# RWKV chunk scan: the next tile's matrix doubling interleaved with this tile's sequential chunks

## The chip, the cores and the metric

The kernel runs on all eight cores of one Trainium2 chip. Each core works through four of the 32 sequences, with no traffic between cores. The metric is the device time of the slowest core in microseconds (us), lower is better. The runs fall into a faster and a slower state: in the slow one a die (cores 0 to 3, or 4 to 7) shows a lower granted TensorE clock and a longer span. In the profiled run of the kernel before, cores 0 to 3 took 20,421 us at clock 0.680 and cores 4 to 7 20,189 us at 0.702 (medians), 1.2% apart. Where I compare stages inside the program, I use the mean over all eight cores of a profiled run.

Engine names: PE is TensorE, PEld its weight loads, DVE is VectorE, ACT is ScalarE. PSUM (`ps_B` in the rows) is the memory that matmuls write; DVE and ACT copy results out of it (a 64x384 copy took 0.49 us on ACT and 0.56 on DVE in the tile shown below). The granted clock is the share of TensorE's full clock that the profile's clock records give. They hold three values: on core 0 in the first profile of the kernel before, 1.0 (full) for 5,502 us, 0.5 (half) for 11,978 us and 0.8125 for 2,877 us.

## The reference, cut to what matters

The model is a two-layer trunk of width 1024 on 2048 tokens. Each layer has three mixers side by side (RWKV-7, retention, band attention), an output projection, and a gated convolution FFN. Only the RWKV mixer's recurrence is concerned here:

```python
def step(state, inp):
    r_t, w_t, k_t, v_t, a_t, b_t = inp
    sa = jnp.einsum('bhvk,bhk->bhv', state, a_t)
    state = (state * w_t[:, :, None, :] + sa[..., None] * b_t[:, :, None, :]
             + v_t[..., None] * k_t[:, :, None, :])
    return state, jnp.einsum('bhvk,bhk->bhv', state, r_t)
```

There are six heads of width 64. The kernel does not step token by token. It takes 64 tokens (a chunk) at a time, inverts a triangular matrix for each chunk, and carries the state from chunk to chunk.

## The kernel before

A block of 512 tokens is four tiles of 128 tokens, two chunks in each. For each tile the scan has three stages in this order. The head pairs (hp) are three, the heads in a pair (hh) two. B[0] to B[7] are the eight PSUM banks. A helper records every instruction and derives waits from the buffers and whole banks that it reads and writes. In the chunks, R sums the right-hand sides, SA multiplies them by N (the inverted matrix), ST is what the chunk adds to the state, and Y is its output.

```python
for t_ in range(NT):
    for hp in range(3):                      # mask stage
        ...                                  # 6 matmuls into B[0..3]
        for hh in range(2):
            tt("dve", LM[hp]..., B[hh][:], msk4[:], ALU.mult, ...)
            tt("dve", LT[hp]..., B[2 + hh][:, 0:128], mskL[:, 0, :], ALU.mult, ...)
        tt("dve", nv, lmv[:, :, 0, :], identbf..., ALU.add, ...)
    bnb = [(7, 0), (7, 256), (3, 256)]
    for lev in range(1, 6):                  # doubling: X -> X*X, N -> N + X*N
        for hp in range(3): ...              # squarings into B[4 + hp]
        for hp in range(3):
            cp("dve" if hp == 1 else "act", xx.ap, B[4 + hp][:], ...)
        for hp in range(3): ...              # N products into bnb[hp]
        for hp in range(3):
            tt("dve", nv, nv, B[bn][:, c0n:c0n + 256]..., ALU.add, ...)
    for hf in range(2):                      # two chunks, one after the other
        ...                                  # R: 12 matmuls into B[7]
        cp("act", rhs_sb.ap[tsl, 0:384], B[7][tsl, 0:384], ...)
        ...                                  # SA: 6 matmuls into B[6]
        cp("dve", sa_sb.ap[tsl, 0:384], B[6][tsl, 0:384], ...)
        ...                                  # ST: 12 matmuls into B[2 + hf]
        ...                                  # Y: 18 matmuls into B[5]
        for hp in range(3):
            stt(S32[l][:, hp, :], ..., B[bsn]..., ...)        # state update, DVE
        put_state(Sn)                        # state to bf16, two ACT copies
        for hp in range(3):
            cp("act", yw[hp]..., B[5]..., ...)
```

The softmax here doesn't subtract the row's maximum and nothing guards it: scores larger than these inputs give would overflow.

## Time and profile before

| what | value | from |
|---|---|---|
| time, 20 runs | 20,485.26 us median (20,262.63 to 20,589.65) | timed runs, among them six of 20,466 us median |
| one scan (first mask multiply to the first head-norm matmul after it) | 111.2 us | trace, mean over 8 cores x 32 scans |
| tile to tile in it | 27.5 us | the same |
| time outside, a pair of successive gaps between scans (one of each layer) | 1046.6 us | the same |
| half clock, share of the scan | 84% | clock records, 8 cores |

One whole tile in the busy table reads as follows (stretch, its length, then busy us and count of PE, PEld, DVE, ACT, POOL; then the granted clock, the DMA share and GB/s):

```profile
7286.22:7313.41 27.19, 18.37 (x198) 12.63 (x198) 16.67 (x45) 8.80 (x22) 0.00 (x0) 0.58 0.01 2
```

PE is busy 68% of it and DVE 61%, so two engines have a third of the tile free. PE's own rows of the second chunk show where its third goes. The bracket is the idle time before the row and what ended it:

```profile
7308.80 0.77 PE L283 MATMUL ps_B<-sb_A 128*64 128x64 bf16 x11 [1.65 <-ACT sb_A L309]
7310.29 0.69 PE L283 MATMUL ps_B<-sb_A 128*64 128x64 bf16 x7 [0.73 <-ACT sb_A L309]
7311.61 1.80 PE L283 MATMUL ps_B<-sb_A 64*64 64x64 bf16 x34 [0.62 <-DVE sb_A L311]
```

Three groups, three waits, and each wait is for a copy that itself waited for PE. From the end of ACT's or DVE's work to PE's start it took 0.14 us at nearly every hand-off of the tile that I followed (once 0.25). These are the holes that the change is meant to fill.

### The profile page before, as it was taken

The numbers are of one execution on the slowest core, as the hardware profiler recorded it, in microseconds if no ns is written. First come the engines' busy times: TensorE is split into PE (matmuls) and PEld (weight loads), VectorE is DVE, ScalarE is ACT, GpSimd is POOL, SyncE is SP. The second block draws the span as 40 slices with busy tenths as digits, with TensorE's granted clock in tenths as the row PEclk, the third lists the DMA queues.
The fourth block names the chain that finished last, engine by engine and source line by source line (L and its number), as shares of the span: only waits on it lengthen the run. The fifth ranks groups of instructions, "written<-read, shape, count | busy, mean of one in ns | idle before, by whom it ended". The sixth has DMA issues, their size and how long they took to land.

```text
span 20427.0 us, 232694 instructions; the slowest of 8 cores (20180.5 to 20427.0 us)
## 1 busy us (share of the span) xinstructions
PE 12774.4 (63%) x69184; PEld 6459.9 (32%) x69792; DVE 10440.2 (51%) x17416; ACT 7718.5 (38%) x18017; POOL 874.5 (4%) x1032
## 2 busy tenths in 40 slices
PE   5666566665666666666556666666655666666665
PEld 2323333232332333323333233332333323333232
DVE  5544554455554455445554445544555544554455
ACT  3343333333334333333333433333333343333333
POOL 0000000000000000000000000000000000000000
PEclk7776666777667666667666766667776676666777
DMA  2243322333224332233322433223332243322332
GB/s 51 46 70 52 57 37 46 67 56 57 40 43 69 52 57 36 46 64 56 55 43 42 70 52 56 37 46 64 54 56 45 42 70 52 57 37 46 64 56 49
DMA packets 1045448, 1069.84 MB, mean 52 GB/s; under 512 B 22912, under 2 KB 990592, under 8 KB 1044224
## 3 DMA queue, kind: packets, MB, share of 16 engines
q0 software_dynamic: 991808, 885.52, 29.2%
q1 hardware_dynamic: 52416, 169.40, 2.5%
q8 instruction: 597, 9.78, 0.2%
q14 instruction: 627, 5.14, 0.1%
HBM read 1906.73 MB, written 33.55 MB: 95 GB/s over the span
## 4 chain that ended last, share of the span: by engine, by line
PE 47%; DVE 19%; issue 14%; ACT 10%; DMA 9%; DVEq 1%; ACTq 0%; SPq 0%; POOLq 0%; POOL 0%
PE ps_B L283 45%; DMA sb_W<-w_up 6%; DVE sb_A L295 5%; ACT sb_A L309 4%; DVE sb_xres L295 3%; ACT sb_xres L292 2%; PE ps_B L286 2%; ACT sb_A L290 2%; DMA sb_W<-w_down 2%; DVE sb_A L304 1%; DVE sb_st L367 1%; DVE sb_st L366 1%; DVE sb_A L311 1%; DMA sb_W<-w_in 1%; ACT sb_A L292 1%
## 5 line engine op out<-in xcount | busy, mean ns | idle before, releaser
L283 PE MATMUL ps_B<-sb_xT,sb_W 128*128 128x512 bf16 x16992 | 4711.0, 442 | 1085.6 <-DMA sb_W<-w_up 810.0
L309 ACT ACTIVATE sb_A<-ps_B 128x512 f32<-128x512 f32 (+6 forms) x5440 | 2436.9, 470 | 4222.6 <-PE ps_B L283 3361.2
L283 PE MATMUL ps_B<-sb_A 64*64 64x64 bf16 (+3 forms) x29952 | 2912.7, 267 | 1617.3 <-DVE sb_A L295 589.4
L283 PEld LDWEIGHTS ps_B<-sb_xT,sb_W 128*128 128x128 bf16 x17408 | 1903.8, 111 | 3894.2 <-issue 2914.9
L304 DVE SCALAR_TENSOR_TENSOR sb_A<-sb_A,sb_cw 128x512 f32<-128x512 f32 x2816 | 2092.4, 750 | 1383.3 <-ACT sb_chal L309 1225.0
L283 PEld LDWEIGHTS ps_B<-sb_A 64*64 64x64 bf16 (+2 forms) x29952 | 1974.1, 134 | 2559.4 <-issue 2333.3
L286 PE MATMUL ps_B<-sb_ident,sb_xres 128*128 128x128 f32 x2560 | 580.8, 403 | 1992.2 <-DVE sb_xres L295 1992.2
L295 DVE TENSOR_TENSOR sb_A<-sb_A 128x512 f32<-128x512 f32 (+1 forms) x2240 | 1476.2, 687 | 495.9 <-ACT sb_A L290 372.4
L283 PE MATMUL ps_B<-sb_W,sb_A 128*128 128x512 bf16 x5504 | 1338.4, 405 | 67.3 <-DMA sb_W<-w_down 51.1
L290 ACT ACTIVATE sb_A<-ps_B 128x128 bf16<-128x128 f32 (+2 forms) x2688 | 872.7, 330 | 1054.8 <-PE ps_B L283 1048.3
L295 DVE TENSOR_TENSOR sb_A<-sb_A,ps_B 128x256 bf16<-128x256 bf16 (+1 forms) x2112 | 826.6, 441 | 782.6 <-PE ps_B L283 771.9
L286 PEld LDWEIGHTS ps_B<-sb_ident,sb_xres 128*128 128x128 f32 x2560 | 467.4, 210 | 2124.2 <-issue 2124.2
L292 ACT ACTIVATE sb_A<-ps_B,sb_cb,sb_cw 128x512 f32<-128x512 f32 x1408 | 1072.5, 762 | 1.7
L311 DVE CAST sb_A<-ps_B 128x512 bf16<-128x512 f32 (+3 forms) x1024 | 619.3, 605 | 865.6 <-PE ps_B L283 692.9
L290 ACT ACTIVATE sb_A<-sb_A 128x512 f32<-128x512 f32 (+1 forms) x1344 | 820.8, 624 | 402.5 <-DVE sb_A L295 287.1
L292 ACT ACTIVATE sb_sd<-sb_mv,sb_epst 128x1 f32<-128x1 f32 x320 | 94.2, 294 | 2295.7 <-DVE sb_mv L368 2295.3
L283 PE MATMUL ps_B<-sb_A,sb_bonesbf 128*128 128x512 bf16 x192 | 107.3, 593 | 1250.6 <-DVE sb_A L304 626.0
L283 PE MATMUL ps_B<-sb_W,sb_yT 128*128 128x512 bf16 x1984 | 550.7, 436 | 537.9 <-DVE sb_yT L295 535.5
L304 DVE SCALAR_TENSOR_TENSOR sb_s_0<-sb_xres,ps_B 128x512 f32<-128x512 f32 x256 | 175.4, 685 | 1366.7 <-PE ps_B L283 1357.9
L500 DVE RECIPROCAL sb_rc<-ps_B 128x4 f32<-128x4 f32 x128 | 23.3, 182 | 1625.9 <-PE ps_B L283 1625.9
L283 PEld LDWEIGHTS ps_B<-sb_W,sb_A 128*128 128x128 bf16 x5632 | 578.0, 103 | 824.6 <-issue 467.9
L134 POOL DMA_DIRECT2D sb_W<-w_up x384 | 335.7, 874 | 9803.3 <-PE ps_B L283 9803.3
(100 smaller groups left out, 13822.3 us busy)
## 6 DMA issues: line engine op xcount, KB each, us to landing
sb_W<-w_up POOLq DMA_DIRECT2D x320, 1024.0 KB, 10.8
sb_W<-w_in POOLq DMA_DIRECT2D x224, 768.0 KB, 8.0
sb_W<-w_down POOLq DMA_DIRECT2D x128, 1024.0 KB, 11.2
sb_W<-w_out POOLq DMA_DIRECT2D x64, 1024.0 KB, 10.9
sb_W<-w_down POOLq DMA_DIRECT2D x64, 768.0 KB, 8.9
sb_lng_t<-lng SPq DMA_DIRECT2D x80, 512.0 KB, 4.7
sb_lnb_t<-lnb SPq DMA_DIRECT2D x80, 512.0 KB, 5.7
sb_W<-w_in POOLq DMA_DIRECT2D x32, 1024.0 KB, 9.8
```

Of the source, the lines that this page charges most:

```text
L134: fn = lambda e, out=out, in_=in_: e.dma_start(out=out, in_=in_)
L283: mk.op("pe", lambda e: e.matmul(out, lhsT=lhsT, rhs=rhs, start=start, stop=stop), reads=r, writes=w)
L286: mk.op("pe", lambda e: e.transpose(out, in_, idn), reads=r, writes=w)
L290: mk.op("act", lambda e: e.activation(out=out, in_=in_, func=func, scale=scale), reads=r, writes=w)
L292: mk.op("act", lambda e: e.activation(out=out, in_=in_, func=func, bias=bias, scale=scale), reads=r, writes=w)
L295: mk.op(eng, lambda e: e.tensor_tensor(out=out, in0=in0, in1=in1, op=op), reads=r, writes=w)
L304: mk.op("dve", lambda e: e.scalar_tensor_tensor(out=out, in0=in0, scalar=scalar, in1=in1, op0=op0, op1=op1), reads=r, writes=w)
L309: mk.op("act", lambda e: e.activation(out=out, in_=in_, func=AF.Copy), reads=r, writes=w)
L311: mk.op(eng, lambda e: e.tensor_copy(out=out, in_=in_), reads=r, writes=w)
L366: mk.op("dve", lambda e: e.bn_stats(out=st_[:, 0, :], in_=s_ap[:, 0:512]), reads=[s_key], writes=[k_])
L367: mk.op("dve", lambda e: e.bn_stats(out=st_[:, 1, :], in_=s_ap[:, 512:1024]), reads=[s_key], writes=[k_])
L500: mk.op("dve", lambda e, POv=POv: e.reciprocal(out=rc[:], in_=POv[:, :, 64:65]), reads=[POk], writes=["rc"])
```

## The change

The intent: while the chunks of tile t hop from engine to engine, let PE, ACT and DVE work on the doubling of tile t+1, which does not depend on them. The three stages become a function and two generators. A small driver takes one step of each generator in turn, and that order is the order of issue.

```diff
+LMs = [LM, [alias_bf(f[6], 0, 2), ...]]     # second set of buffers, on dead ones
+LTs = [LT, [...]]
+Nms = [Nm, [...]]
+def mat(t_): ...                            # mask stage, as before
+def gen_dbl(t_):                            # yields after: squarings, copies, N products, N adds
 ...
-  bn, c0n = bnb[hp]
+  bn = 4 + hp                               # N product in the squaring's own bank
 ...
+def gen_seq(t_):                            # yields after each of 8 steps of a chunk
 ...
-  mm(B[6][tsl, ...], nv..., rhs_sb..., ...)  # SA
+  mm(B[7][tsl, ...], nv..., rhs_sb..., ...)
-  o_ = B[5][po:po + 64, ...]                 # Y
+  o_ = B[0][po:po + 64, ...]
 ...
+def run_interleaved(gens): ...              # next() on each in turn until all are done
+mat(0)
+run_interleaved([gen_dbl(0)])
+for t_ in range(NT):
+    if t_ + 1 < NT:
+        mat(t_ + 1)
+        run_interleaved([gen_seq(t_), gen_dbl(t_ + 1)])
+    else:
+        run_interleaved([gen_seq(t_)])
```

The banks had to be dealt out anew, as two stages are alive at once: doubling keeps 4 to 6, chunks take 7, 2 or 3, and 0.

## The prediction

> **What bounds the kernel now.** I read the first lines of the page, then the busy times by stretch, then the timeline of each engine over one step of the RWKV scan, because the change touches nothing else.
>
> ```profile
> span 20427.0 us, 232694 instructions; the slowest of 8 cores (20180.5 to 20427.0 us)
> PE 12774.4 (63%) x69184; PEld 6459.9 (32%) x69792; DVE 10440.2 (51%) x17416; ACT 7718.5 (38%) x18017; POOL 874.5 (4%) x1032
> ```
>
> No engine is full over the whole. The program runs 4 sequences x 4 blocks x 2 layers = 32 layer-blocks, each with one scan of four 128-token tiles. The first mask multiply (sb_msk on DVE) of a scan starts it and the first head-norm matmul (sb_bones on PE) after it ends it. Over all 32 scans of this core that gives 111.06 us a scan (109.7 to 112.3), 3554 us in all, **17.4% of the span**. So the change can only act on 17.4%, and 2% of the time (409 us) means 12.8 us a scan. Tile to tile is 27.46 us in the mean, and the end of the last tile to the first head-norm matmul adds 1.2 us.
>
> Busy times in one tile (stretch in us, then us and count of PE, PEld, DVE, ACT, POOL; then the granted clock). The rows are the mask stage, the doubling, and the two sequential chunks:
>
> ```profile
> 7286.22:7291.68 5.46, 4.04 (x22) 2.05 (x23) 5.46 (x17) 1.77 (x6) 0.00 (x0) 0.50 0.00 0
> 7291.68:7303.32 11.64, 8.59 (x76) 6.08 (x77) 8.24 (x21) 4.88 (x9) 0.00 (x0) 0.67 0.01 2
> 7303.32:7313.41 10.09, 5.74 (x101) 4.50 (x101) 2.97 (x10) 2.15 (x7) 0.00 (x0) 0.52 0.01 2
> ```
>
> The mask stage is DVE bound (5.46 of 5.46). In the chunks nobody is: DVE 2.97 and ACT 2.15 of 10.09. That is a chain of hand-offs. The timeline (start, length, engine, operation) of ACT and then DVE in the second chunk shows it:
>
> ```profile
> 7309.66 0.49 ACT L309 ACTIVATE sb_A<-ps_B 64x384 bf16<-64x384 f32 x1 [0.53 <-PE ps_B L283]
> 7313.51 0.81 ACT L309 ACTIVATE sb_A<-sb_S_1 64x192 bf16<-64x192 f32 x2 [3.36 <-DVE sb_S_1 L304]
> 7314.35 0.46 ACT L309 ACTIVATE sb_A<-ps_B 128x64 f32<-128x64 f32 x3
> ...
> 7310.90 0.56 DVE L311 CAST sb_A<-ps_B 64x384 bf16<-64x384 f32 x1 [3.15 <-PE ps_B L283]
> 7312.37 1.05 DVE L304 SCALAR_TENSOR_TENSOR sb_S_1<-sb_S_1,sb_pcs,ps_B 128x64 f32<-128x64 f32 x3 [0.91 <-PE ps_B L283]
> ```
>
> With the PE rows: right-hand-side matmuls R (12) at 7308.80, ACT copy at 7309.66, SA matmuls (6) at 7310.29, DVE copy at 7310.90, state matmuls ST (12) at 7311.61, state update at 7312.37, state to bf16 at 7313.51 until 7314.32. The hand-offs are R to copy 0.87, copy end to PE 0.14, SA to copy 0.60, ST to update 0.77. A chunk is thus 0.87+0.49+0.14+0.60+0.55+0.14+0.77+1.05+0.10+0.81+0.14 = 5.66 us.
>
> [...] The three rows above agree that there is room: doubling plus chunks have 11.2 us of DVE in 21.7. [...] I lay the streams out by hand in that order. [...] The clock records of this trace hold only 0.5 and 1.0, and average 0.575 in the scans. [...]
>
> **The change part by part.**
> (a) No arithmetic is added or removed: the same matmuls, copies and adds per tile. ACT and DVE work is only reordered, the PE stream too.
> (b) A second set of mask and doubling buffers lies on dead projection buffers. No copies or transfers come from it.
> (c) The mask stage of tile t+1 moves ahead of the chunks of tile t. It still takes 5.5 us of DVE, but the first chunk's R can start when PE has issued the last mask matmuls, some 4.4 us after the first mask multiply (the third pair's matmuls wait for the second pair's banks, read out at about 3.7 us, plus 0.7). So 1.1 us of it hides.
> (d) The N product moves into the squaring's own bank, so the next squaring now waits for the N add. Alone, a level is then S, copy, N, add in a ring. The last head pair needs matmuls 0.44, hand-off 0.18, copy 0.60, 0.15, matmuls 0.22, 0.2, add 0.36, 0.15 = 2.3 us, with queueing about 2.45. Before, N adds start 2.79, 2.41, 2.23 and 1.96 us apart in this tile. So the unhidden first doubling stays about as it was.
> (e) The overlap. Eight steps of a chunk meet eight steps of doubling, that is two levels. PE's order is R, S, SA, N, ST, S, Y, N. Half clock, 0.11 us per 128-column matmul, R at 0:
> - R 0 to 0.77, S to 2.1. Copy of R 0.87 to 1.36, squaring copies ACT 1.39 to 1.99 and 2.28 to 2.88, DVE 1.84 to 2.53.
> - SA waits behind S: 2.1 to 2.5. DVE copy 2.7 to 3.25, N adds 3.25 to 4.33.
> - ST 3.39 to 4.1. Second S to 5.43. Its DVE copy stands ahead of the state update in DVE's queue: 5.17 to 5.86.
> - Y 5.43 to 6.5. Update 5.86 to 6.9, state to bf16 7.0 to 7.8, next R at 7.95. The second N adds end at 8.03, no hindrance.
>
> So a chunk stretches from 5.66 to **7.95 us** (0.6 from SA behind S, 1.7 from the update behind the second copy) and carries two levels, worth 4.9 us alone.
> (f) The fifth level has no partner: chunks have 16 steps, doubling 20. Laid out the same way it adds 2.3 us.
>
> Tile period after: 4.4 + 7.95 + 7.95 + 2.3 = 22.6 us against 27.8 for a half-clock tile before (the first scan has tiles of 27.81). One scan: first mask stage and doubling alone 17.4 (mask start to last N add, first tile), three such periods 67.8, last chunks alone 11.0. Sum **96.2 us against 111.06**, 14.9 us less. The schedule is for half clock throughout. The real mix made a tile 27.46 and not 27.8, so I take 1.3% off the rest: 95.0 us. Saving 16.0 us x 32 = **515 us, 2.5%**.
>
> **The rivals.**
> 1. The two chains disturb each other more than laid out, a wait in place of the one removed. For: [...] And PE is close to full at half clock: its eight groups sum to 7.0 us of the 7.95 (DVE 5.1, ACT 4.2). Against: the layout has these waits in it already, and its steps are measured ones. One microsecond more per overlapped chunk is 6 us a scan, 190 us in all: about 20,140, inside 2%.
> 2. The overlap is nearly free, and DVE becomes the bound: 16.67 us of DVE per tile is the floor, 5.9 us below my 22.6. Half of that gap closed is 9 us a scan, 280 us: 19,670. Denser PE work could also raise the clock in the scan. Against: in the attention stage (9615 to 9660 us) PE is busy 0.85 to 0.88 and the clock still 0.50, so density alone did not do it there; and at half clock PE itself has some 18 us of issue in a tile (the 14.0 of two chunks, 1.3 of the fifth level, about 3 of the mask stage).
> 3. The time comes back outside. For: stages outside run at 0.70 (this die) against 0.73 (other die), and that die difference alone is 1.2% of the span. Against: outside stages keep their order, and in the 559.06 us after one scan the DMA share is 0.38, against 0.01 in the scan, so transfers hidden by the scan are few. I allow 100 us either way.
> 4. The scan hidden behind something else: no, every engine finishes the scan before head-norm, so its length is on the path.
>
> **Range and chances.** From 20,466 less 515: 19,950 us. Saving per scan between 9 and 23 us, with 0.5% of scatter of the runs (20,263 to 20,577 already), gives 19,710 to 20,180. The 2% line is at 12.8 us a scan, 3.2 below my figure, and my error is about 5 to 6 either way: 0.70 faster, 0.29 within 2%, 0.01 slower.
>
> **What would show it.** Tile period in the scan near 22.3 us and scan near 95; mask stage still 5.5 us of DVE; the time from one state-to-bf16 copy to the next near 8 us where overlapped and 5.7 in the last tile; DVE's update of the state coming right behind a 128x512 CAST with no idle time; a lone fifth level of about 2.3 us; stages outside unchanged within 1%. The prediction fails if the chunk step is above 9 us (PE held by waits on banks 4 to 6) or under 7, or if the clock in the scan leaves 0.5 to 0.65.

The layout in (e) runs each engine's instructions in the order of issue. That was my assumption when I made it. The order of one pair on DVE was varied later: the scan took 86.4 us with the state update ahead of the copy and 90.2 us with it behind.

## The result, and the profile after

The changed kernel took **19,797.39 us** (median of 10 runs, 19,740.44 to 19,919.61). Its ratio to the kernel before is **0.9684**, 95% interval 0.9641 to 0.9728. A ratio here is the mean time of one kernel's fast runs over that of the other's fast runs of the same rounds, so it is not quite the ratio of the medians above. Two later sets on other occasions gave 0.971 and 0.9667.

First lines of the page:

```profile
span 19706.0 us, 233334 instructions; the slowest of 8 cores (19581.5 to 19706.0 us)
PE 12468.8 (63%) x69792; PEld 6227.4 (32%) x69792; DVE 10433.8 (53%) x17416; ACT 7718.7 (39%) x18017; POOL 874.7 (4%) x1032
```

DVE and ACT have the same counts and the same work as before (DVE 10,440 and 10,434 us); only the span shrank. By the traces, the scan went from 111.2 to **90.3 us**, and the pair of gaps outside from 1046.6 to 1047.1 us. So 20.9 us x 32 = 669 us were won inside the scans. The medians differ by 688 us.

That the two means of the gaps agree is in part chance, because a slow profile is compared with a fast one. Before, a pair took 1053 to 1054 us on the slow die (15 to 17% of the time outside at clock 0.8125) and 1038 to 1040 us on the other (none of it); in the changed kernel it took 1043 to 1051 us (5 to 11%). Over the four profiles without the new banks (this one, the two fillers and the repeat below), a pair is about 1039 us plus 105 us times that share, and the three profiles of the changed kernel lie 0 to 2.5 us under this line in the mean. So nothing came back outside that the share at 0.8125 does not account for. Whether the change raises that share is not shown.

On the two dies of the profile before, a scan took 111.1 to 111.4 us on every core, while their spans were 1.2% apart. A second profile of the kernel before gave 111.2 us again (below).

The busy table of one tile of the changed kernel, cut where ACT starts to write the new state (first mask multiply to first state copy; to second state copy; to the next tile):

```profile
7759.67:7770.56 10.89, 9.54 (x99) 6.78 (x97) 9.23 (x25) 2.88 (x5) 0.00 (x0) 0.50 0.01 2
7770.56:7778.01 7.45, 6.20 (x84) 4.72 (x84) 4.77 (x13) 4.06 (x11) 0.00 (x0) 0.64 0.01 3
7778.01:7781.12 3.11, 1.88 (x18) 1.00 (x18) 2.32 (x7) 1.73 (x7) 0.00 (x0) 0.81 0.00 0
```

The stages with separate limits are gone: in the first stretch DVE is busy 85% (mask stage and the first chunk under it) and PE 88%. PE's timeline shows the same as long runs:

```profile
7762.30 8.41 PE L283 MATMUL ps_B<-sb_A 64*128 64x256 bf16 x91 [0.31 <-DVE sb_A L295]
7771.52 6.10 PE L283 MATMUL ps_B<-sb_A 128*64 128x64 bf16 x83 [0.81 <-ACT sb_A L309]
```

Where PE stopped three times a chunk, it now stops once, for the state. What is left on the way is in DVE's and ACT's rows:

```profile
7768.82 0.69 DVE L311 CAST sb_A<-ps_B 128x512 bf16<-128x512 f32 x1 [0.76 <-PE ps_B L283]
7769.43 1.04 DVE L304 SCALAR_TENSOR_TENSOR sb_S_0<-sb_S_0,sb_pcs,ps_B 128x64 f32<-128x64 f32 x3
...
7770.56 0.82 ACT L309 ACTIVATE sb_A<-sb_S_0 64x192 bf16<-64x192 f32 x2 [0.73 <-DVE sb_S_0 L304]
...
7778.01 0.82 ACT L309 ACTIVATE sb_A<-sb_S_0 64x192 bf16<-64x192 f32 x2 [0.82 <-DVE sb_S_0 L304]
```

The state update has no idle time before it and stands right behind the doubling's 128x512 CAST, as the prediction said it would.

The clock also moved. By the clock records of the eight cores, 59% of the scan ran at half clock, against 84% before; outside the scans it was 54% in both. Over 512 overlapped tiles (eight cores, the second and third period of each scan) the mean clock was 0.746, against 0.570 in the same tiles before. The tile of the busy table above, at 0.60, is one of the slower ones.

The time of one tile follows its clock closely in both kernels. I sorted the tiles by mean clock:

| mean clock of the tile | before: tiles, mean us | changed: tiles, mean us |
|---|---|---|
| 0.50 | 97, 27.96 | none |
| 0.50 to 0.60 | 251, 27.56 | 9, 21.71 |
| 0.60 to 0.70 | 164, 27.15 | 100, 21.29 |
| 0.70 to 0.80 | none | 233, 20.91 |
| 0.80 to 0.90 | none | 170, 20.26 |
| straight line, at clock 0.5 | 27.96 | 22.32 |

The line at half clock is 22.32 us, an extrapolation, as no tile's clock was that low, and the prediction's layout at half clock was 22.6.

### The profile page after: what moved, and what is told of

Its sections match the earlier page's. It is cut to its first block, busy times and chain, and to the rows that moved or that the text cites. A ratio compares the mean times of both kernels' runs of the same rounds, so it can differ in the third digit from the quotient of the medians.

```text
span 19706.0 us, 233334 instructions; the slowest of 8 cores (19581.5 to 19706.0 us)
## 1 busy us (share of the span) xinstructions
PE 12468.8 (63%) x69792; PEld 6227.4 (32%) x69792; DVE 10433.8 (53%) x17416; ACT 7718.7 (39%) x18017; POOL 874.7 (4%) x1032
## 4 chain that ended last, share of the span: by engine, by line
PE 47%; DVE 18%; issue 14%; DMA 10%; ACT 10%; DVEq 1%; ACTq 0%; SPq 0%; POOLq 0%
PE ps_B L283 45%; DMA sb_W<-w_up 7%; DVE sb_A L295 5%; ACT sb_A L309 4%; DVE sb_xres L295 3%; ACT sb_xres L292 2%; PE ps_B L286 2%; ACT sb_A L290 2%; DMA sb_W<-w_down 1%; DVE sb_A L304 1%; DVE sb_st L367 1%; DVE sb_st L366 1%; DMA sb_W<-w_in 1%; ACT sb_A L292 1%; DVE sb_xT L311 1%
## 5 line engine op out<-in xcount | busy, mean ns | idle before, releaser
L283 PE MATMUL ps_B<-sb_A 64*64 64x64 bf16 (+4 forms) x29952 | 2678.5, 250 | 1177.5 <-DVE sb_A L295 538.9
L283 PEld LDWEIGHTS ps_B<-sb_A 64*64 64x64 bf16 (+3 forms) x29952 | 1786.4, 123 | 2073.0 <-issue 1710.1
```

Source lines behind the costliest of these rows:

```text
L283: mk.op("pe", lambda e: e.matmul(out, lhsT=lhsT, rhs=rhs, start=start, stop=stop), reads=r, writes=w)
```

## The experiments

All outputs are right. "Scan" is the mean over eight cores. Ratios are to the kernel before, run on the same chip in the same rounds.

**All the new parts, but no overlap.** The driver runs the three stages of one tile in turn.

```diff
-mat(0)
-run_interleaved([gen_dbl(0)])
-for t_ in range(NT): ... run_interleaved([gen_seq(t_), gen_dbl(t_ + 1)]) ...
+for t_ in range(NT):
+    mat(t_)
+    run_interleaved([gen_dbl(t_)])
+    run_interleaved([gen_seq(t_)])
```

> The changed kernel's code, buffers and banks, but the generators run one after another: mask stage, doubling, chunks of the same tile. Theory (the gain is all overlap): tile period 27.5 us and scan 111 us as in the kernel before, ratio to it 0.995 to 1.005, clock in the scan 0.57. Rival (the new banks or buffers themselves gain or cost): ratio off 1 by over 0.5%.

Measured: tile 29.2 us, scan 116.2 us, ratio 1.0156 (1.0074 to 1.0237). The rival was right: the new parts cost 1.7 us a tile when nothing covers them. (5.0 us x 32 = 160 us is 0.8% of the time; the rest of the ratio is noise or lies outside the scans, where the profiled run spent 17 to 31% at clock 0.8125.) At the end of a tile, ACT's last row, then PE's and DVE's first of the next mask stage:

```profile
7471.80 0.46 ACT L309 ACTIVATE sb_A<-ps_B 128x64 f32<-128x64 f32 x3
...
7472.40 0.72 PE L283 MATMUL ps_B<-sb_A 64*128 64x256 bf16 x6 [2.18 <-ACT sb_A L309]
...
7473.09 0.69 DVE L295 TENSOR_TENSOR sb_A<-ps_B,sb_msk 128x512 bf16<-128x512 f32 x1 [2.22 <-PE ps_B L283]
```

PE stands 2.18 us until ACT has copied Y out, because Y now lies in bank 0, which the mask stage writes first. Before, Y lay in bank 5, and DVE went on from the state update to the mask stage with no idle time:

```profile
7312.37 1.05 DVE L304 SCALAR_TENSOR_TENSOR sb_S_1<-sb_S_1,sb_pcs,ps_B 128x64 f32<-128x64 f32 x3 [0.91 <-PE ps_B L283]
7313.41 0.69 DVE L295 TENSOR_TENSOR sb_A<-ps_B,sb_msk 128x512 bf16<-128x512 f32 x1
```

In the changed kernel the four last doubling steps lie between the two, so the cost is hidden. The overlap thus wins more than the net: 116.2 less 90.3, or 25.9 us a scan, of which 5.0 only pay for the new parts that it needs.

**The mask stage ahead, chunks and doubling one after the other.**

```diff
-        run_interleaved([gen_seq(t_), gen_dbl(t_ + 1)])
+        run_interleaved([gen_seq(t_)])
+        run_interleaved([gen_dbl(t_ + 1)])
```

> The changed kernel with only the mask stage of the next tile ahead of the chunks, and chunks and doubling not interleaved. Theory: R starts 4.4 us after the first mask multiply instead of waiting for 5.5 us, so 1.1 us less in each of three tiles, scan about 108 us, ratio to the kernel before 0.993 to 0.998; the interleaving of chunks and doubling is the other 17 us. Rival (the hoist is much of the gain): scan under 103 us, ratio under 0.988.

Measured: scan 111.8 us, tile 27.8 us, ratio 0.9921 (0.9783 to 1.006), which settles nothing; the scan does. Neither number came: the hoist (the mask stage moved ahead) with the new banks is no faster than the kernel before (111.8 against 111.2). It did start R early, but ACT gave some of that back at the other end:

```profile
7210.47 0.81 ACT L309 ACTIVATE sb_A<-sb_S 64x192 bf16<-64x192 f32 x2 [3.37 <-DVE sb_S L304]
7211.31 1.44 ACT L309 ACTIVATE sb_A<-ps_B 128x64 f32<-128x64 f32 x5
```

The row of five holds the three Y copies and the first two squaring copies of the next doubling, which ran behind the state copies on ACT. Against the run in turn, which has the same buffers and banks, the hoist does win 4.4 us (116.2 to 111.8), about what the banks cost (5.0). The interleaving wins the other 21.5 us (111.8 to 90.3). Together that is the net 20.9.

**Filler on PE in the kernel before.** To see whether the clock, and through it the tile, follows the amount of matmul work, I put matmuls whose result nobody reads in PE's waits. In the first kernel:

```diff
+def fill(bank):
+    mm(B[bank][:], identbf[:], btT[0].ap, True, True, ...)   # 128x512
 ...
 cp("act", rhs_sb..., B[7]..., ...)
+fill(0)
 cp("dve", sa_sb..., B[6]..., ...)
+fill(1)
 put_state(Sn)
+if hf == 0: fill(0); fill(1)
```

> The kernel before with up to four 128x512 matmuls per chunk that nobody reads, put where PE waits (after R, after SA, two after Y), to raise PE's activity and change nothing else. Theory (the clock in the scan follows PE activity, and the clock is the 6 us a scan that the prediction missed): clock in the scan rises from 0.57 to 0.65 or more and the tile follows the line 27.96 - 6.46 x (clock - 0.5) fitted over the tiles of the kernel before, so about 26.7 us at 0.70; scan 107 to 109 us, ratio to the kernel before 0.994 to 0.998. Rival (the clock does not follow from the scan's own density, or the tiles' relation to clock is only coincidence): clock stays at 0.57, or rises and the tile stays at 27.5 or above.

Measured: clock of the tiles 0.558, tile 27.54 us, scan 111.5 us, median of four timed runs 20,661 us against 20,648 of seven. The clock did not rise.

The second has 128-column matmuls with dense weights, five after R, six after SA, eight after Y of the first chunk, and four in each of two mask groups:

> The kernel before with more and denser matmuls that nobody reads, 128 columns with dense weights as the doubling has them, in the chunk waits and in the mask stage: 25,600 columns a tile in place of 20,736, a mean of 0.78 of half-clock streaming in place of 0.63 (0.71 in the first filler, 0.83 in the changed kernel). Theory (clock follows density of real work): clock in the scan at 0.62 or more and the tile on the fitted line, 27.2 us or less. Rival (what raises the clock in the changed kernel is not mean density but stretches of back-to-back matmuls without the chain's pauses): clock stays at 0.55 to 0.59 and the tile at 27.4 or more.

Measured: clock 0.575, tile 27.47 us, scan 111.1 us, ratio 1.0013 (0.9935 to 1.009). Again no rise. One tile of it in the busy table:

```profile
7356.11:7383.25 27.14, 22.42 (x236) 15.70 (x236) 16.73 (x45) 8.76 (x22) 0.00 (x0) 0.63 0.01 2
```

PE is busy 22.42 of 27.14 us, 83%. Over all 512 tiles PE is busy 85% here, 80% with the first filler and 78% in the changed kernel, yet the mean clocks are 0.575, 0.558 and 0.746. By the columns counted in the expectation above, the dense filler streams 25,600 in 27.47 us (932 a us) and the changed kernel 20,736 in 20.78 us (998 a us); in the kernel before it was 20,736 in 27.51 us (754 a us), at clock 0.570. The same filler in the mask stage of the changed kernel (nine matmuls a tile):

> The changed kernel with nine 128x128 matmuls that nobody reads in each mask stage, where PE waits for DVE. Theory ([...] the tile follows the line 22.4 - 6.5 x (clock - 0.5)): clock of the overlapped tiles 0.80 or more, tile 20.4 us or less. Rival (as in the two fillers of the kernel before, filler does not count): clock 0.75, tile 20.8 us or, where the filler delays R, more.

Measured: clock 0.750 (0.746 without it), tile 20.73 us, scan 90.3 us, ratio 0.9672. No rise either. So PE's busy share and the mean amount of matmul work do not explain the clock. The changed kernel has longer unbroken runs of PE (8.41 and 6.10 us in the rows above; the longest was 4.13 us in the tile of the kernel before and 4.92 us in the filler's), but no run here varied that alone. What raised the clock is not shown.

**The kernel before again**, for a second profile beside these:

> The kernel before once more, for a profile beside the others on the same chip, if possible in the fast state: scan 111 us, tile 27.5 us, clock in the scan 0.57, whatever the die. If instead the scan of a fast run is shorter than 109 us, part of the difference read from the first pair of traces was state, not change.

Measured: scan 111.2 us, clock in it 0.574, tile 27.5 us. The run was slow again (spans 20,264 to 20,595 us), with the other die the slow one this time, and the scan the same. The state shows outside the scan: in the first profile of before, the slow die spent 16% of its time outside the scans at clock 0.8125, the other none of it; here it was 19% and 5%.

**The changed kernel again**, as the measure for its neighbours, with three rounds:

> The changed kernel as it is, on the same chip as the next three, as their measure: ratio to the kernel before 0.964 to 0.973, scan 90 us, overlapped tile 20.8 us, clock in the scan 0.70.

Measured: ratio 0.971 (0.9645 to 0.9776), scan 90.3 us, tile 20.78 us. And with five rounds:

> The changed kernel again with five rounds, as the measure for the next two on this chip: ratio to the kernel before 0.966 to 0.972.

Measured: ratio 0.9667 (0.9614 to 0.9721), scan 90.2 us.

**Own banks for the N product.** Does the next squaring lose time to the N add in the shared bank?

```diff
-bn = 4 + hp
+bn, c0n = [(1, 0), (1, 256), (2 if lev in (3, 4) else 3, 256)][hp]
```

> The changed kernel with the N products in banks of their own again (1, 1 and the free half of 2 or 3), so that the next squaring no longer waits for the N add. Theory (in the overlapped layout ST and the state copy hold PE longer than the N adds do): tile 20.6 to 21.0 us, scan 89.5 to 91 us, same ratio as the changed kernel within 0.3%. Rival (the shared bank holds back the squarings): tile under 20.2 us, scan under 88 us.

Measured: tile 20.90 us, scan 90.3 us, ratio 0.9682 against 0.971 of the changed kernel beside it (intervals overlap widely). The shared bank costs nothing here.

**The state update ahead of the copy.** One `yield` moves, so that DVE gets the update before the second squaring's copy.

```diff
-yield
 for hp in range(3):
     stt(S32[l][:, hp, :], ...)
+yield
 put_state(Sn)
```

> The changed kernel with the state update issued one step earlier, so that on DVE it stands ahead of the second squaring's copy instead of behind it. Theory (the update behind that copy stretches each overlapped chunk): about 0.7 us less in each of six chunks, overlapped tile about 19.4 us, scan about 86 us, ratio to the kernel before 0.961 to 0.964, that is 0.6% under the changed kernel. Rival (ACT or PE sets the chunk anyway): tile stays at 20.5 us or more.

Measured: tile 19.33 us, scan 86.6 us, ratio 0.9654 (0.9569 to 0.9738). The scan is as expected; the time could not tell it from the changed kernel, and the stages outside spent about a quarter of their time at clock 0.8125 in the profiled run. So it ran again, five rounds:

> The version with the state update ahead of the second copy again, five rounds beside the changed kernel. By the scans (86.6 against 90.3 us, 3.7 us x 32 = 118 us of 20,500) its ratio to the kernel before should be 0.006 under that of the changed kernel. If the stages outside give it back through a lower clock, the difference is under 0.002 although the scan stays at 86.6.

Measured: ratio **0.9586** (0.9538 to 0.9634) against 0.9667 (0.9614 to 0.9721) of the changed kernel on the same chip, median 19,799.42 us against 19,956.99. The intervals still overlap a little; the scans do not: 86.4 against 90.2 us in two kernels that differ in one line. DVE and ACT in a second chunk:

```profile
7157.30 1.08 DVE L295 TENSOR_TENSOR sb_A<-sb_A,ps_B 128x256 bf16<-128x256 bf16 x3
7158.30 1.04 DVE L304 SCALAR_TENSOR_TENSOR sb_S<-sb_S,sb_pcs,ps_B 128x64 f32<-128x64 f32 x3
7159.26 0.68 DVE L311 CAST sb_A<-ps_B 128x512 bf16<-128x512 f32 x1
...
7158.35 1.26 ACT L309 ACTIVATE sb_A<-ps_B 128x512 bf16<-128x512 f32 x2 [1.30 <-PE ps_B L283]
7159.63 0.81 ACT L309 ACTIVATE sb_A<-sb_S 64x192 bf16<-64x192 f32 x2
```

The update now runs before the CAST. From first to second state copy it is 5.86 us in the mean, where the changed kernel has 6.9 to 7.0 and a chunk with nothing beside it (the last) 5.71. So two levels of doubling ride along in the second chunk for little, but not like for like: the last chunk ran at half clock throughout, this one at 0.97. The stretch from second state copy to the next tile grew from 3.1 to 3.5 us. This version is the best that ran.

**The mask stage under the last doubling steps.** On top of that, the mask groups of tile t+2 go between the four doubling steps that have no chunk beside them.

> As the last, and the mask stage of the tile after next is issued between the last four doubling steps, which have no chunk step beside them. Theory (that tail is a chain with DVE idle for 1 to 1.5 us of it): 1 us less in two tiles of a scan, tile 18.3 to 18.8 us, scan 84 to 85.5 us, ratio 0.002 under the last. Rival (the last N add, now behind two mask groups on DVE, holds the next chunk's SA): tile 19.3 us or more.

Measured: ratio 0.9652 (0.9594 to 0.971), scan 87.0 us. The rival was right. The interval from first mask multiply to the next was 18.97 us in the mean, but it starts earlier in the tile now; summed from state copy to state copy in the steady tile it is 2.44 + 11.25 + 5.93 = 19.6 us against 3.46 + 9.96 + 5.86 = 19.3. DVE shows why:

```profile
7148.51 1.07 DVE L295 TENSOR_TENSOR sb_A<-sb_A,ps_B 128x256 bf16<-128x256 bf16 x3
7149.50 0.68 DVE L295 TENSOR_TENSOR sb_A<-ps_B,sb_msk 128x512 bf16<-128x512 f32 x1
...
7152.47 0.55 DVE L311 CAST sb_A<-ps_B 64x384 bf16<-64x384 f32 x1 [0.50 <-PE ps_B L283]
```

The mask stage is full on DVE, so the fifth level's copy and adds only lengthen it, and the third mask group, and with it the first chunk's SA copy (64x384), comes later by as much.

## Why the prediction was right or wrong

The verdict (faster) and the range were right. The saving was under-sized: 515 us predicted, 669 us by the scans.

- **No work added, no time given back outside.** Right: the same DVE and ACT counts, gaps outside 1046.6 and 1047.1 us a pair.
- **Mask stage 5.5 us of DVE, R under its tail.** Right in kind; R starts a little earlier. From first mask multiply to first state copy the layout had 4.4 + 7.0 = 11.4 us. The tiles whose stretch ran wholly at half clock took 10.95, 0.45 us less than laid out.
- **The chunk step of 7.95 us.** Near for the clock that it was made for: over the tiles, a line through the time between the two state copies against its clock gives 7.95 us at 0.5. That is an extrapolation; the nine stretches below clock 0.6 took 7.74. But that stretch ran at a mean clock of 0.857 and took 6.98 us; stretches wholly at full clock took 6.60. So the step fell just under the 7 us that the prediction named as a sign of being wrong.
- **The unpaired fifth level.** From second state copy to the next tile, the layout had 10.25 - 7.0 = 3.25 us; measured 3.13.
- **The unhidden first doubling as before.** Right: 17.25 us for the first period, 17.4 laid out. The last chunk took 5.71 us, 5.66 predicted.
- **The update behind the second copy costs 1.7 us of a chunk at half clock.** Right in kind; moving it ahead won 1.1 us in the second chunk and 0.7 in the stretch up to the first.
- **The term that was mis-sized is the clock.** The prediction laid out "half clock throughout" and took "1.3% off" for the real mix, named a scan clock outside 0.5 to 0.65 as what would make it fail, and argued that density alone would not raise it. The scan's clock was 0.70, its overlapped tiles' 0.746. So by its own signs the prediction failed on the clock, and its range (9 to 23 us a scan) was wide enough to hold the 20.9. The sum shows how much that was: 96.2 laid out against 90.3 measured is 5.9 us. In each of three periods the clock is 0.98 in the second chunk, 0.28 in the first stretch (10.95 to 10.67) and about 0.1 in the tail, so 4.1 us; the early R is 3 x 0.45 = 1.35; the first period and the end give the rest, about 0.45. I had allowed 1.2 us for the clock.
- **Rival 2 came true in part.** The clock rose. The reason given against it, that density alone does not raise the clock, also held for PE's busy share: three fillers left the clock where it was (0.558 and 0.575 against 0.570, 0.750 against 0.746). What raised it in the overlapped tiles is not shown.
- **"Only 0.5 and 1.0" was a wrong reading.** The clock records of that same trace also hold 0.8125. Outside the scans of the slow die it was 16% of the time.
- **Rival 1**, chains that disturb each other more, did not come; the order of one pair on DVE was the only disturbance worth a repair.

## What to carry to other kernels

When two chains are interleaved on the same engines, write down the order of issue on each engine, and put the step that the serial chain waits for ahead of the other chain's copy: one moved line was worth 3.8 us of a 90 us scan. Lay the schedule out with measured durations, but state the clock that it is for: here the same matmuls were granted 0.570 in the tiles before and 0.746 when overlapped. Filling idle PE time with unread matmuls did not raise the clock here (0.558 and 0.575). New bank assignments can cost time of their own (1.7 us a tile here), so run the new buffers without the overlap as a control.
